# Rows of the late modulation read through GpSimd's DMA queue, and each sum written one part later

## The chip, the cores and the metric

The kernel runs on one core of a Trainium2 chip. The metric is the device time of one execution in microseconds. Three executions of the kernel before took 1044.27, 1046.89 and 1050.75 us; their median is 1046.89 us.

## The reference

One trunk layer of a diffusion backbone: 512 latent tokens and 256 context tokens of width 1024 are modulated, go through two attention branches (latent attention with 8 heads, differential attention with 4), a gated merge and an output projection, a layer norm, and then a routed mixture of 16 experts with a second layer norm. What matters here is the modulation vector:

```
mod = jax.nn.silu(c) @ w_ada[l] + b_ada[l]
sh1, sc1, g1, sh2, sc2, g2 = jnp.split(mod[:, None, :], 6, axis=-1)
...
x = layer_norm(DEEPNORM_ALPHA * x + g1 * o_lat, ln1_g[l], ln1_b[l])
x = layer_norm(DEEPNORM_ALPHA * x + g2 * ec_moe(x * (1.0 + sc2) + sh2, *moe), ln2_g[l], ln2_b[l])
```

w_ada is a 1024 x 6144 matrix in float32. Its first two sixths (sh1, sc1) are needed before anything else. The other four (g1, sh2, sc2, g2) are needed only after the attention; the kernel calls for them later, and they are the "late modulation" of this document.

## The kernel before, in words

**Startup.** The x and ctx tokens are transposed and modulated in four quarters of 256 channels. For each quarter q, `mod_load` (L218) issues on SyncE's queue (SP) the two pieces of w_ada (L222 and L223, tile `wa`, 1 MB each), the tokens (L226, L227, tile `xq`) and the first weight piece of the input projection (L196, tile `wraw`, 512 KB). `mod_mul` (L230) multiplies on TensorE (PE; L237) and VectorE (DVE) copies the result (L240, tile `ms`); `mod_t` turns it into columns (L247 and L250, tiles `scv` and `shv`); `x_chunk` modulates a channel block (L261, tile `xtmp`) and splits it into a high part on ScalarE (ACT; `xlh`, L75) and a low part on GpSimd (POOL; `xll`, L78). Then PE multiplies each block with three passes (L82, L83, L84).

**Projection.** The input projection is done in chunks of up to 512 columns (`chunk`, L362, and `gates`, L447). Each of the four steps of a chunk loads a `wraw` page on SP, splits it into `whi` (ACT) and `wlo` (DVE) and multiplies. Between matmuls the chunks call `mod_chunk` 32 times: 8 times in the chunk C_DV, 12 times in gates(0) and 12 times in gates(1) (table `MOD_AT`, L39).

**Late modulation.** It is done on DVE. A part is one block of 128 rows of w_ada and 1024 columns (512 KB, tile `wa2`, shown as `wa_739`, `wa_760` and so on in the orders below). Each part is scaled by its column of silu(c) and added to the running total of the part before (L348; the first part of a sixth by L346). Eight parts give a sixth, and there are four such sixths, 32 parts. After the eighth part `mod_sum` (L353) sums over the 128 rows with four matmuls on PE (L358), loads 64 KB rows of b_ada into a further `wa2` buffer (L359, two DMAs) and adds them on DVE into `rm` (L360). There are three `wa2` buffers (N_WA, L39), for the parts and for the b_ada rows alike. A buffer comes free when its last reader is done: for most parts that is the DVE operation of the next part, for the eighth part of a sixth it is the sum on PE.

**What sets the order.** Up to the attention the framework's scheduler orders each engine's instructions; it may move an instruction past others that it doesn't depend on. Each engine and each DMA queue then runs its own list strictly in order: what stands behind a waiting instruction waits too. In the kernel before, `wraw` pages and `wa2` parts are issued from the same list, SP's. The emission calls of `mod_chunk` first write the sum that is due, then the next part.

**After it.** `mod_end` (L584) transposes `rm` (L589); then come gates(2), gates(3), the attention, the output projection and the experts. From about 520 us on the experts' weights fill the DMA engines.

Of the kernel before, what the change touches and what calls it, by code (L numbers as in the profile page):

```python
# [18 lines left out]
D = 1024  # L19
# [5 lines left out]
KD = D // 128  # L25
# [27 lines left out]
def _layer(tc, A, out, opened):  # L53
    nc = tc.nc
    V, S, G, T = nc.vector, nc.scalar, nc.gpsimd, nc.tensor
    dma = nc.sync.dma_start
# [129 lines left out]
    w_ada = A["w_ada"][0].rearrange("(k p) n -> p k n", p=128)  # L186
# [144 lines left out]
    b_ada = A["b_ada"][0].rearrange("(j n) -> j n", n=512)  # L331
    wrt = mw.tile([128, KD, E_N], F32, name="wrt")
    halves, late = [], []

    def mod_chunk():

        for fn in late:
            fn()
        late.clear()
        if len(halves) == 4 * KD:  # L340
            return
        j, k = divmod(len(halves), KD)
        wa = mw.tile([128, D], F32, name="wa2", bufs=N_WA)
        dma(wa, w_ada[:, k, (2 + j) * D:(3 + j) * D])
        if k == 0:
            V.tensor_scalar(wa, wa, cs[:, 0, 0:1], None, op0=OP.mult)  # L346
        else:
            V.scalar_tensor_tensor(wa, wa, cs[:, k, 0:1], halves[-1], op0=OP.mult, op1=OP.add)  # L348
        halves.append(wa)
        if k == KD - 1:  # L350
            late.append(lambda: mod_sum(j, wa))

    def mod_sum(j, wa):  # L353
        i, h = divmod(j, 2)
        pm = psa.tile([128, 512], F32, name="tp", bufs=2)
        bm = mw.tile([128, D], F32, name="wa2", bufs=N_WA)
        for g in (2 * h, 2 * h + 1):
            T.matmul(pm[32 * g:32 * g + 32, :], one2[:, 0:1].to_broadcast([128, 32]), wa[:, (g % 2) * 512:(g % 2) * 512 + 512], start=True, stop=True)  # L358
            dma(bm[32 * g:32 * g + 32, :512], b_ada[4 + 4 * i + g:5 + 4 * i + g].to_broadcast([32, 512]))  # L359
        V.tensor_tensor(rm[i][64 * h:64 * h + 64], pm[64 * h:64 * h + 64], bm[64 * h:64 * h + 64, :512], op=OP.add)  # L360

    def chunk(col, n, cuts, evac, at, nxt):  # L362
# [257 lines left out]
    while len(halves) < 4 * KD or late:  # L620
        mod_chunk()
# [276 lines left out]
    for c in range(4):  # L898
        hl = wos[c]
        for jj in range(2):  # L900
            j = 2 * c + jj
            ps = psc.tile([128, 512], F32, name="om", bufs=3)
            wo_mul(ps, hl, jj, oM)
            g = yt.tile([128, 512], F32, name="gy")
# [485 lines left out]
```

## Time and profile before

| | |
|---|---|
| median of three runs | 1046.89 us |
| the profiled execution's own time | 1044.37 us |
| its span, first to last instruction | 1042.6 us |
| mean granted TensorE clock | 0.986 of full speed |
| PE busy | 980.1 us (94% of the span) |
| DVE busy | 447.2 us (43%) |
| ACT busy | 278.3 us (27%) |
| POOL busy | 173.4 us (17%) |
| w_ada parts of the late modulation | 32 DMAs of 512 KB on SP, median 4.6 us to landing |

Issuing a DMA from SP isn't counted as busy time; "to landing" is the time from the start of the issue to the arrival of the last byte's signal. A granted clock of 1.00 is the 2.4 GHz level; a stretch with 0.92 ran partly at 1.2 GHz. A busy time of PE includes the overlap of pipelined matmuls, so a full PE may be below its peak.

### The profile page before, as it was taken

What the parts mean: (1) busy time and instruction counts of PE and PEld (TensorE: products, weight loads), DVE (VectorE), ACT (ScalarE), POOL (GpSimd) and SP (SyncE); (2) the same over time, 40 slices, a digit from 0 to 9 for tenths busy, and PEclk for the clock granted to TensorE, in tenths of its full rate; (3) what the DMA queues carried; (4) which work ended last, traced back from release to release, by engine and by line L of the source; (5) the groups of instructions that cost most, each with busy time, mean ns of one, the idle gap of its engine ahead of it and who ended that gap; (6) DMA issues with size and microseconds to landing.
All of it is one profiled execution on the core that took longest, in us unless ns stands there. A gap on an engine that the chain in (4) does not pass through costs nothing.

```text
span 1042.6 us, 13825 instructions
## 1 busy us (share of the span) xinstructions
PE 980.1 (94%) x5280; PEld 615.3 (59%) x5280; DVE 447.2 (43%) x871; ACT 278.3 (27%) x556; POOL 173.4 (17%) x176
## 2 busy tenths in 40 slices
PE   6999999999989999999996999999999999999982
PEld 5888977768778777777764443535353534234331
DVE  2382366662678555558473312221313131111227
ACT  1222325224777555544110101010101010010010
POOL 2340020202677322210021400000000000000004
PEclk9999999999999999999998999999999999999997
DMA  9944347752111100038948989999999999999993
GB/s 299 289 157 131 96 119 257 239 189 78 27 35 57 41 1 21 21 99 300 406 161 325 376 303 408 409 409 409 409 408 409 409 409 409 409 409 409 410 371 118
DMA packets 101210, 266.98 MB, mean 256 GB/s; under 512 B 14020, under 2 KB 37528, under 8 KB 101144
## 3 DMA queue, kind: packets, MB, share of 16 engines
q1 hardware_dynamic: 100248, 264.52, 68.2%
q0 software_dynamic: 320, 1.05, 0.3%
q8 instruction: 42, 0.69, 0.3%
q10 hardware_dynamic: 576, 0.52, 0.1%
q14 instruction: 24, 0.20, 0.1%
HBM read 261.47 MB, written 2.10 MB: 253 GB/s over the span
## 4 chain that ended last, share of the span: by engine, by line
PE 70%; DMA 10%; issue 9%; DVE 5%; POOL 2%; ACT 2%; SPq 0%; POOLq 0%; DVEq 0%; ACTq 0%
PE h L1179 15%; PE y L1195 8%; PE mx L1142 6%; PE acc L82 5%; PE acc L84 5%; PE acc L83 5%; DMA wr<-moe_w 5%; PE sc L653 4%; DMA wa<-w_ada 3%; PE tpb L661 3%; PE av L841 3%; PE mx L1208 2%; PE po L84 1%; PE po L83 1%; PE po L82 1%
## 5 line engine op out<-in xcount | busy, mean ns | idle before, releaser
L1179 PE MATMUL h<-wr,xe 128*64 128x512 f32 x1024 | 233.6, 598 | 8.9 <-DMA wr<-moe_w 7.9
L1179 PEld LDWEIGHTS h<-wr,xe 128*64 128x64 f32 x1024 | 68.2, 136 | 163.0 <-issue 106.6
L1195 PE MATMUL y<-wr,hidT 128*64 128x512 f32 x448 | 97.7, 594 | 0.0
L642 DVE TENSOR_REDUCE nm<-sc 128x1 f32<-128x768 f32 x64 | 61.0, 953 | 34.4 <-PE sc L653 33.8
L1182 DVE TENSOR_TENSOR hid<-hid,h 128x512 f32<-128x512 f32 x16 | 11.0, 688 | 147.8 <-PE h L1179 147.8
L1195 PEld LDWEIGHTS y<-wr,hidT 128*64 128x64 f32 x448 | 31.5, 137 | 61.8 <-issue 58.2
L1154 POOL TENSOR_TENSOR oh<-oh,aff 128x512 f32<-128x512 f32 x8 | 8.4, 1048 | 350.2 <-PE mx L1142 350.2
L643 ACT ACTIVATE P<-sc,nm 128x768 f32<-128x768 f32 x64 | 57.6, 901 | 31.8 <-DVE nm L642 22.7
L1142 PE MATMUL mx<-oh,xn 128*128 128x128 f32 x512 | 60.4, 280 | 1.4 <-DVE oh L1132 1.4
L1142 PEld LDWEIGHTS mx<-oh,xn 128*128 128x128 f32 x512 | 59.4, 196 | 2.5 <-issue 1.3
L75 ACT ACTIVATE whi<-wraw 128x1024 fp32r<-128x1024 f32 (+1 forms) x32 | 33.5, 1046 | 100.8 <-DMA wraw<-w_in 76.8
L78 DVE TENSOR_TENSOR wlo<-wraw,whi 128x1024 fp32r<-128x1024 f32 (+1 forms) x32 | 38.7, 1209 | 45.0 <-PE acc L83 29.1
L75 ACT ACTIVATE ye<-y 128x512 fp32r<-128x512 f32 (+2 forms) x17 | 9.7, 572 | 178.1 <-DVE y L1202 98.7
L82 PE MATMUL acc<-xlh,whi 128*128 128x512 f32 x128 | 51.6, 403 | 2.8 <-ACT whi L75 2.0
L1209 DVE TENSOR_TENSOR acc<-acc,mx 128x512 f32<-128x512 f32 x56 | 34.7, 680 | 41.4 <-PE mx L1208 41.4
L1181 ACT ACTIVATE hid<-h 128x512 f32<-128x512 f32 x16 | 9.6, 597 | 154.9 <-PE h L1179 154.9
L83 PE MATMUL acc<-xll,whi 128*128 128x512 f32 x128 | 50.8, 397 | 0.0
L82 PE MATMUL acc<-whi,xlh 128*128 128x512 f32 (+1 forms) x128 | 49.5, 391 | 1.0 <-ACT whi L75 1.0
L84 PE MATMUL acc<-xlh,wlo 128*128 128x512 f32 x128 | 50.0, 398 | 0.0
L1202 DVE SCALAR_TENSOR_TENSOR y<-y,gate,g2b 128x512 f32<-128x512 f32 x14 | 9.9, 754 | 92.6 <-PE y L1195 92.6
L84 PE MATMUL acc<-whi,xll 128*128 128x512 f32 (+1 forms) x128 | 48.7, 381 | 0.5 <-POOL xll L78 0.5
L83 PE MATMUL acc<-wlo,xlh 128*128 128x512 f32 (+1 forms) x128 | 48.8, 381 | 0.2 <-DVE wlo L78 0.2
(341 smaller groups left out, 1704.4 us busy)
## 6 DMA issues: line engine op xcount, KB each, us to landing
wr<-moe_w SPq DMA_DIRECT2D x372, 512.0 KB, 10.2
wa<-w_ada SPq DMA_DIRECT2D x32, 512.0 KB, 4.6
wraw<-w_in SPq DMA_DIRECT2D x28, 512.0 KB, 4.8
wa<-w_ada SPq DMA_DIRECT2D x8, 1024.0 KB, 9.8
wr<-moe_w SPq DMA_DIRECT2D x16, 384.0 KB, 8.4
outraw<-w_out SPq DMA_DIRECT2D x8, 512.0 KB, 11.1
xq<-x SPq DMA_DIRECT2D x4, 512.0 KB, 7.8
q<-q SPq DMA_DIRECT2D x16, 128.0 KB, 2.3
```

Source lines behind the costliest of these rows:

```text
L75: S.activation(hi, src, AF.Copy)
L78: (eng_lo or V).tensor_tensor(lo, src, f(hi), op=OP.subtract)
L82: T.matmul(ps, lh, rh, start=start, stop=False)
L83: T.matmul(ps, lh, rl, start=False, stop=False)
L84: T.matmul(ps, ll, rh, start=False, stop=stop)
L642: V.tensor_reduce(nm, ps[:, :768], axis=AX.X, op=OP.max, negate=True)
L643: S.activation(p, ps[:, :768], AF.Exp, bias=nm, accum_out=z)
L653: T.matmul(ps[:, a:b], l, r[:, a:b], start=i == 0, stop=i == len(passes) - 1)
L1142: T.matmul(pss[hf][:, kk * 128:(kk + 1) * 128], xn[t][:, k * 128:(k + 1) * 128], o[:, t].rearrange("p e s -> p (e s)"), start=t == 0, stop ...
L1179: T.matmul(ph[i][64 * hf:64 * hf + 64, :], xe[:, k, sl], w[:, hf * 512:(hf + 1) * 512], start=k == 0, stop=k == KD - 1)
L1195: T.matmul(py[hf][r0:r0 + 64, :], hT[:, e % 2, fc % 4, fc // 4, :], w[:, hf * 512:(hf + 1) * 512], start=fc == 0, stop=fc == KD - 1)
L1209: V.tensor_tensor(acc[t][:, hs], acc[t][:, hs], ps, op=OP.add)
```

## The change

`mod_chunk` now writes the next part first and the sum that was due after it, so a sum is written one part later than before. The 32 loads of parts (512 KB each) and the 8 loads of b_ada rows are issued from GpSimd's queue instead of SP's. Nothing else differs.

```
     def mod_chunk():
 
-        for fn in late:
+        due = late[:]
+        late.clear()
+        if len(halves) < 4 * KD:
+            mod_part()
+        for fn in due:
             fn()
-        late.clear()
-        if len(halves) == 4 * KD:
-            return
+
+    def mod_part():
         j, k = divmod(len(halves), KD)
         wa = mw.tile([128, D], F32, name="wa2", bufs=N_WA)
-        dma(wa, w_ada[:, k, (2 + j) * D:(3 + j) * D])
+        G.dma_start(wa, w_ada[:, k, (2 + j) * D:(3 + j) * D])
         if k == 0:
             V.tensor_scalar(wa, wa, cs[:, 0, 0:1], None, op0=OP.mult)
         else:
...
-            dma(bm[32 * g:32 * g + 32, :512], b_ada[4 + 4 * i + g:5 + 4 * i + g].to_broadcast([32, 512]))
+            G.dma_start(bm[32 * g:32 * g + 32, :512], b_ada[4 + 4 * i + g:5 + 4 * i + g].to_broadcast([32, 512]))
```

From this place on the line numbers of the changed kernel are 3 higher: L346 and L348 become L349 and L351, the load L344 becomes L347, the sum L358 becomes L361.

The scheduler puts the instructions elsewhere. DVE's list at the start of the program, before; `cs` is silu(c), `ms`, `vecs`, `scv`, `shv` and `xtmp` belong to the first quarter of the startup:

```order
L168 TENSOR_SCALAR cs<-sg 128x8
L169 TENSOR_SCALAR cs<-sg 128x8
L240 COPY ms<-tp 128x128
L183 COPY vecs<-tp 128x68
L184 TENSOR_SCALAR gsub<-vecs 128x1
L247 SCALAR_TENSOR_TENSOR scv<-tp,vecs 128x4
L250 TENSOR_TENSOR shv<-tp,vecs 128x4
```

And the same place in the changed kernel:

```order
L169 TENSOR_SCALAR cs<-sg 128x8
L349 TENSOR_SCALAR wa_739<-wa_739,cs 128x1024
L351 SCALAR_TENSOR_TENSOR wa_760<-wa_760,cs,wa_739 128x1024
L240 COPY ms<-tp 128x128
L183 COPY vecs<-tp 128x68
L351 SCALAR_TENSOR_TENSOR wa_787<-wa_787,cs,wa_760 128x1024
L184 TENSOR_SCALAR gsub<-vecs 128x1
L247 SCALAR_TENSOR_TENSOR scv<-tp,vecs 128x4
```

The first two parts of the late modulation now stand ahead of `ms`, the third ahead of `scv`; six more (up to `wa_904` and `wa_1366`, the first part of the next sixth) stand among the second quarter's and ahead of the third quarter's `ms`. Before, the first part stood behind all four quarters.

DVE's list at the second quarter in the changed kernel, where four of these parts stand among the quarter's own steps:

```order
L351 SCALAR_TENSOR_TENSOR wa_808<-wa_808,cs,wa_787 128x1024
L351 SCALAR_TENSOR_TENSOR wa_835<-wa_835,cs,wa_808 128x1024
L240 COPY ms<-tp 128x128
L351 SCALAR_TENSOR_TENSOR wa_856<-wa_856,cs,wa_835 128x1024
L247 SCALAR_TENSOR_TENSOR scv<-tp,vecs 128x4
L250 TENSOR_TENSOR shv<-tp,vecs 128x4
L351 SCALAR_TENSOR_TENSOR wa_883<-wa_883,cs,wa_856 128x1024
L261 TENSOR_SCALAR xtmp<-tp,scv,shv 128x512
```

In the kernel before, these rows hold `ms`, `scv`, `shv` and `xtmp` alone.

SP's list before, around the end of the second sixth (parts up to `wa_1460`, its b_ada rows in `wa_1476`, then the third sixth from `wa_1482`):

```order
L344 DMA wa_1451<-w_ada 128x1024
L471 DMA wuq<-mla_w_uq 128x768
L196 DMA wraw<-w_in 128x2x512
L344 DMA wa_1460<-w_ada 128x1024
L359 DMA wa_1476<-b_ada 32x512 x2
L344 DMA wa_1482<-w_ada 128x1024
L344 DMA wa_1497<-w_ada 128x1024
```

POOL's list in the changed kernel at the same place (the third sixth begins with `wa_1475`, the b_ada rows are in `wa_1479`; `qtok` are short additions of the latent queries):

```order
L347 DMA wa_1451<-w_ada 128x1024
L347 DMA wa_1460<-w_ada 128x1024
L347 DMA wa_1475<-w_ada 128x1024
L362 DMA wa_1479<-b_ada 32x512 x2
L347 DMA wa_1497<-w_ada 128x1024
L347 DMA wa_1506<-w_ada 128x1024
L502 TENSOR_TENSOR qtok<-q1t,q2t 128x2x32 x2
L347 DMA wa_1521<-w_ada 128x1024
```

The weight loads (`wraw`, `wuq`) no longer stand among the parts. The two b_ada loads now come behind the first part of the next sixth, and so take the buffer that the DVE operation of `wa_1460` frees.

## Rows read from the trace of the kernel before

**Rows 1.** Busy time by stretch of the span (its header names the columns).
```profile
core 0: us, PE busy (x) PEld busy (x) DVE busy (x) ACT busy (x) POOL busy (x), PEclk, DMA share, GB/s
0.00:26.00 26.00, 17.10 (x167) 13.96 (x168) 6.53 (x22) 4.32 (x7) 6.18 (x13) 1.00 0.92 299
26.00:52.00 26.00, 25.53 (x223) 21.02 (x222) 8.41 (x16) 7.11 (x11) 8.86 (x8) 1.00 0.98 289
52.00:143.00 91.00, 91.00 (x449) 79.01 (x449) 43.52 (x70) 26.56 (x55) 16.91 (x17) 1.00 0.41 124
143.00:160.00 17.00, 17.00 (x83) 13.22 (x81) 13.26 (x20) 4.66 (x7) 3.80 (x6) 1.00 0.52 160
160.00:180.00 20.00, 18.29 (x84) 14.51 (x83) 13.46 (x21) 10.98 (x39) 0.14 (x1) 1.00 0.74 257
180.00:200.00 20.00, 19.19 (x89) 15.62 (x90) 15.39 (x43) 4.75 (x13) 6.58 (x16) 1.00 0.70 237
200.00:212.00 12.00, 9.97 (x41) 7.24 (x40) 6.49 (x7) 3.87 (x6) 0.00 (x0) 0.97 0.76 245
212.00:230.00 18.00, 18.00 (x77) 13.65 (x76) 11.40 (x16) 4.21 (x6) 1.15 (x1) 0.92 0.69 223
```

**Rows 2.** Chain that ended last, in order of time: start us, us, what.
```profile
150.11 0.98 PE tp L358 x4
...
152.16 4.59 DMA wa<-w_ada
156.84 1.30 DVE wa L348
...
168.60 4.83 DMA wa<-w_ada
173.52 1.29 DVE wa L348
174.86 1.05 PE tp L358 x4
...
225.21 0.98 PE tp L358 x4
```

**Rows 3.** What SP's queue waited for, 0 to 260 us: total us, times, longest.
```profile
SPq L344 <- DVE wa L348: 56.3, 21, 6.3
SPq L344 <- PE tp L358: 9.0, 3, 7.0
```

**Rows 4.** What PE waited for, 140 to 262 us: total us, times, longest.
```profile
PE acc L82 <- ACT whi L75: 2.0, 1, 2.0
PE tp L358 <- DVE wa L348: 1.5, 1, 1.5
```

**Rows 5.** Operations on tile wa: ns min/median/max, first and last start, forms.
```profile
L348 DVE SCALAR_TENSOR_TENSOR wa<-wa,cs,wa x28: 1276/1285/1758, 62.9 to 223.6; 128x1024 f32<-128x1024 f32 x28
```

**Rows 6.** Line L344, the parts' loads on SP: issue to landing.
```profile
DMA to landing us min/median/max: 3.5/4.6/5.0
```

**Rows 7.** DVE in order of time, startup: start, us, instruction, idle before it.
```profile
11.90 0.29 DVE L240 COPY ms<-tp 128x128 f32<-128x128 f32 x1 [7.98 <-PE tp L237]
12.62 0.16 DVE L247 SCALAR_TENSOR_TENSOR scv<-tp,vecs 128x4 f32<-128x4 f32 x1
24.81 0.29 DVE L240 COPY ms<-tp 128x128 f32<-128x128 f32 x1 [7.11 <-PE tp L237]
27.71 1.48 DVE L261 TENSOR_SCALAR xtmp<-tp,scv,shv 128x512 f32<-128x512 f32 x2 [0.97 <-PE tp L258]
29.11 1.22 DVE L78 TENSOR_TENSOR wlo<-wraw,whi 128x1024 fp32r<-128x1024 f32 x1
```

**Rows 8.** Line L1217, the only loads issued from POOL (256 KB each).
```profile
L1217 POOL DMA_DIRECT2D gb<-ln_g x2: 589/673/757, 565.6 to 571.8; - x2
L1217 POOL DMA_DIRECT2D gb<-ln_b x2: 546/552/559, 566.4 to 572.4; - x2
...
DMA to landing us min/median/max: 6.1/6.5/7.8
```

**Rows 9.** POOL in order of time, startup.
```profile
14.64 1.27 POOL L78 TENSOR_TENSOR xll<-xtmp,xlh 128x512 fp32r<-128x512 f32 x1 [12.72 <-ACT xlh L75]
...
29.26 2.20 POOL L78 TENSOR_TENSOR xll<-xtmp,xlh 128x512 fp32r<-128x512 f32 x1 [9.72 <-ACT xlh L75]
```

## The prediction, made before the changed kernel ran

> **What bounds the kernel now.** I first read the busy time by stretch [rows 1]. Three regimes are to be seen there up to 230 us. From 0 to 52 us the DMA engines are busy 0.92 and 0.98 of the time at 299 and 289 GB/s, and PE lacks 8.9 us of the first stretch: the startup waits for transfers. From 52 to 160 us PE is full. From 160 to 212 us PE lacks 1.71 + 0.81 + 2.03 = 4.55 us, and from 200 to 230 us its granted clock is 0.97 and 0.92, part of the time at the lower of its two levels, which costs 12 x 0.03 + 18 x 0.08 = 1.8 us. What could be won by a better late modulation is therefore about 6.3 us: nothing before 160 us has a gap but the startup.
>
> The chain that ended last says what the gap is [rows 2]. Between the first sum of the late modulation (150.11 us) and the last (225.21 us), 75.1 us, it runs through loads of parts and their DVE operations: 4.59 us, 1.30 us, later 4.83 us, 1.29 us, then the sum on PE. The waits agree: SP's queue stood 56.3 us over the parts' loads until a DVE operation freed a buffer, and 9.0 us until a sum freed one [rows 3], while PE itself waited 1.5 us for a sum's input and 2.0 us for a split weight page [rows 4]. So the late stretch has its own clockwork, with three buffers: a load may start when the operation two parts earlier is done. Two parts take a landing and an operation.
>
> Its size can be checked. From one sum to the next there are four such links, of a landing of 4.6 us (the median of these loads [rows 6]) and an operation of 1.285 us [rows 5], and about 1 us for the sum [rows 2]: 4 x 5.9 + 1 = 24.6 us. Three intervals make 73.7 us, against 75.1 us seen. PE's own work in this stretch is a little less than that, so the clockwork and PE run almost together. The landing time of a part is thus the quantity that decides: 12 landings stand one behind the other.
>
> **The change: the startup.** With its own queue, the first part no longer waits behind SP's list. The order shows nine parts, 9 x 0.524 = 4.7 MB, ahead of or among the first three quarters of the startup, where DVE had none. DVE runs in order, so what matters is not only whose bytes go first. The copy `ms` of the first quarter can't run until the operations of two parts are done, and `scv` not until a third is. Whatever the share of the two queues, 3 x 0.524 = 1.57 MB more must have landed by then. At 299 GB/s [rows 1] that is 5.3 us. The first two operations fit in the 7.98 us in which DVE waits before `ms` [rows 7]; the third lies between `vecs` and `scv`, on the path to the first `xtmp`: 1.3 us. In the second quarter `ms` came at 24.81 us and `xtmp` at 27.71 us [rows 7]; two more operations stand between them, one of which fits beside the transposes PE does there, the other not: 1.3 us. Loads four to seven must land in the some 13 us between the two `ms`; I count them as hidden by PE's work on the first quarter. Sum: 5.3 + 1.3 + 1.3 = 7.9 us. PE has no gap from 26 to 160 us but 0.47 us [rows 1], so nothing gives this back. The bounds: at least the 1.3 us of the third operation, if the loads fitted in idle DMA time; that is 0.08 x 26 + 0.02 x 26 = 2.6 us of it in 52 us, 0.8 MB, so they don't. At most all nine loads in series, 4.7 MB at 299 GB/s, 15.8 us.
>
> **The change: the middle.** The DVE operations and loads that leave the stretch from 52 to 143 us lay beside a full PE [rows 1]; I count 0.
>
> **The change: the late stretch.** The nine early parts don't start the clockwork earlier. The eleventh load takes over either a buffer that the first sum on PE reads or one freed after it, and that sum keeps its place in the last part of PE's work before 151 us. So 23 parts remain between the first and the last sum, with the same three buffers, and the same 12 landings in series. Two terms change.
>
> First, the landing of a load issued from POOL. The only ones in the trace are four loads of half the size, in the stretch in which the expert weights flow: 6.1 to 7.8 us [rows 8]. The nearest on the other side are the parts' own loads on SP: 3.5 us at best, 4.6 us in the median [rows 6]. So a landing lies between 3.5 and 7.8 us. The new queue has no weight page ahead of a part, and the stretch's DMA share is 0.69 to 0.76 [rows 1], not full as at the expert weights; but the issue alone holds POOL for 0.55 to 0.76 us [rows 8]. I take the middle of 4.6 and 6.1 us, 5.35 us: 12 x 0.75 = 9.0 us more.
>
> The Trainium skill speaks for less. Its page "DMA: Bandwidth & Descriptors", section "Anatomy of one DMA — SWDGE (gpsimd) path", gives 2.0 us plus bytes over 436 GB/s for a DMA issued from GpSimd, an estimate of 3.2 us for a part. By it the first rival below would hold. The trace does not agree where it shows such loads: 6.1 us for 256 KB [rows 8].
>
> Second, the b_ada loads. Before, they were issued while the eighth part was still on its way. Now the sum is written a part later, and they wait for the buffer that the eighth part's operation frees; the next sixth's second load stands behind both of them on POOL. Two issues of 0.6 us [rows 8] at two of the sums: 2.4 us. The additions `qtok` also stand behind loads on POOL now, but their readers come in the attention.
>
> What is removed: a weight page no longer waits on SP behind a part, so PE's 2.0 us for a split page goes [rows 4]. What is late next is the sum, whose wait grows by the same amount. I count 0, as I do for the 4.55 us of gaps: they return only if the clockwork gets shorter than PE's work.
>
> **The sum.** 7.9 + 9.0 + 2.4 = 19.3 us. Added to the profiled execution's own time, 1044.37 us (its span of 1042.6 us and 1.8 us around it), this gives 1063.7 us; I say 1064 us. That execution is 2.5 us below the median of the three runs, well inside their spread. The later stages start with what the attention leaves and run as before, so the shift carries through to the end. With a startup of 5 to 10 us and a landing of 4.6 to 6.1 us this case runs from 1044.4 + 5 + 0 + 2.4 = 1052 to 1044.4 + 10 + 18 + 2.4 = 1075 us.
>
> **The rivals.** *Not slower: the freed queue makes the clockwork shorter than PE's work.* Place: the parts' loads between the sums. If a landing is the 3.5 us of the quiet loads [rows 6], an interval is 4 x 4.8 + 1 + 1.2 = 21.4 us, while PE's busy time between the sums is about 23.5 us ([rows 1]: 18.29 + 19.19 in 40 us, and 9.97 in 12). PE then bounds it and gets back 6.3 us; with the startup's 7.9 us that is 1046 us, and if the startup's loads hid as well, 1038 us. It decides from a landing under about 4.0 us. For it: the new queue holds no weight pages. Against it: [rows 8].
>
> *Only the startup pays.* A part lands as on SP, 4.6 us, and the b_ada loads hide: 1044.4 + 7.9 = 1052 us. For it: the check of the clockwork above, which needs nothing else. Against it: POOL's issues are longer than SP's.
>
> *Much slower: POOL's loads are held up.* With the 7.8 us of [rows 8] as landing the late stretch grows by 12 x 3.2 = 38 us, 1093 us with the rest. A mechanism for it is seen at the startup: POOL's low part took 2.20 us instead of 1.27 us [rows 9] where DVE's `wlo`, with two inputs in SBUF, ran beside it from 29.11 us [rows 7]. The operation of a part has two such inputs as well. If each of the 12 issues in series were held for one operation, that is 12 x 1.3 = 15 us on top of the forecast, 1079 us. The Trainium skill's page "SBUF — State Buffer" has the rule ("DVE blocks DMA", and section "Who interferes with whom"): DVE and GpSimd share a port pair, and descriptors of a GpSimd DMA wait for it. It limits the clash for two-input operations to GpSimd instructions that read SBUF; no run here shows descriptors written beside one.
>
> *The change doesn't do what it says.* The sums are written later, but the scheduler places three of the four a few matmuls earlier on PE, not later; so what the later writing does is only the b_ada term, already counted.
>
> **How the numbers follow.** A measurement of this kernel tells about 1% from no change, that is under 1036.4 or over 1057.4 us against the median. My forecast has 0.52, only the startup 0.17, not slower 0.15, much slower 0.16. Of the forecast about 0.44 lies over 1057.4 us, with much slower 0.16 and 0.02 of the second rival: 0.62. Faster by over 1% needs both the whole 6.3 us and a free startup: 0.03. The rest, 0.35, is within 1%. The range leaves out most of the much slower case and half of the not slower one: 1048 to 1080 us.
>
> **What would show it.** In the changed profile: L349 and the first L351 before the first `ms`, with DVE waiting for them or `ms` later than 11.90 us by some 5 us, and the second quarter's `xtmp` at about 36 us; DMA share near 1 until after 50 us; PE full from there to the first sum, now at about 158 us; landings of L347 near 5.4 us; first to last sum about 86 us instead of 75.1; POOL as the releaser of DVE's waits. I am wrong if the first sum still comes by 152 us (startup hidden), or if the stretch between the sums is no longer than 75 us.

## The result, and the profile after

The changed kernel takes 1065.15 us in the median of four executions (1060.49 to 1066.07 us), the kernel before 1046.2 us in the median of four beside it. The ratio is 1.0155, with a 95% interval of 1.0128 to 1.0183: slower by 1.3 to 1.8%. Its profiled execution took 1065.24 us with a span of 1063.2 us, 20.6 us above that of before; the mean granted TensorE clock is 0.977 of full speed where it was 0.986.

Four marks in PE's timeline divide the loss. "First scores" is the first product of queries and keys after the projections.

| us from the start | before | after | later by | added here |
|---|---|---|---|---|
| first sum of the late modulation | 150.1 | 158.1 | 8.0 | 8.0 |
| last sum | 225.2 | 238.7 | 13.5 | 5.5 |
| first scores | 262.4 | 280.1 | 17.7 | 4.2 |
| scores of the other branch (L653, L656) | 330.6 | 349.8 | 19.2 | 1.5 |
| end of the span | 1042.6 | 1063.2 | 20.6 | 1.4 |

So 17.7 us are lost before the attention, in two places: the startup, and the stretch of the late modulation. Some 3 us come later, and no run here was made for them.

**The startup.** Busy time by stretch of the changed kernel, answering to [rows 1]:

```profile
core 0: us, PE busy (x) PEld busy (x) DVE busy (x) ACT busy (x) POOL busy (x), PEclk, DMA share, GB/s
0.00:26.00 26.00, 13.39 (x99) 10.26 (x101) 10.70 (x26) 4.43 (x7) 9.18 (x18) 1.00 0.94 324
26.00:52.00 26.00, 23.68 (x205) 19.30 (x206) 13.28 (x19) 5.19 (x8) 8.90 (x12) 0.93 1.07 361
52.00:143.00 91.00, 91.00 (x500) 79.30 (x499) 29.30 (x55) 26.84 (x56) 17.04 (x18) 1.00 0.32 85
...
160.00:180.00 20.00, 19.18 (x85) 15.46 (x83) 12.81 (x13) 8.36 (x21) 3.58 (x8) 1.00 0.89 317
180.00:200.00 20.00, 15.94 (x67) 13.01 (x67) 11.64 (x30) 7.94 (x33) 6.21 (x13) 0.83 0.54 175
...
230.00:245.00 15.00, 9.76 (x36) 6.41 (x35) 8.02 (x7) 1.06 (x1) 2.09 (x4) 0.77 0.41 138
```

The DMA engines were nearly full before, at 299 and 289 GB/s; now they bring 324 and 361 GB/s, and still PE is busy 3.7 us less in the first 26 us and 1.9 us less in the next; there its granted clock is also 0.93 instead of 1.00, which is worth 26 x 0.07 = 1.8 us. These three make 7.4 of the 8.0 us. After 52 us PE is full again, with nothing given back. The later lines show where PE falls behind a second time: 4.1 us idle in the 20 us from 180 us, 5.2 us in the 15 us from 230 us, both with the granted clock partly at the lower level (0.83 and 0.77).

VectorE in the first two quarters of the startup of the changed kernel, answering to [rows 7] (start, us, instruction, idle before it and its releaser):

```profile
7.82 0.75 DVE L349 TENSOR_SCALAR wa<-wa,cs 128x1024 f32<-128x1024 f32 x1 [3.91 <-DMA wa<-w_ada]
9.89 1.28 DVE L351 SCALAR_TENSOR_TENSOR wa<-wa,cs,wa 128x1024 f32<-128x1024 f32 x1 [1.32 <-DMA wa<-w_ada]
16.42 0.29 DVE L240 COPY ms<-tp 128x128 f32<-128x128 f32 x1 [5.25 <-PE tp L237]
16.77 1.28 DVE L351 SCALAR_TENSOR_TENSOR wa<-wa,cs,wa 128x1024 f32<-128x1024 f32 x1
18.02 0.15 DVE L247 SCALAR_TENSOR_TENSOR scv<-tp,vecs 128x4 f32<-128x4 f32 x1
...
29.25 0.29 DVE L240 COPY ms<-tp 128x128 f32<-128x128 f32 x1 [1.85 <-PE tp L237]
33.51 1.29 DVE L351 SCALAR_TENSOR_TENSOR wa<-wa,cs,wa 128x1024 f32<-128x1024 f32 x1 [3.96 <-DMA wa<-w_ada]
...
35.23 1.28 DVE L351 SCALAR_TENSOR_TENSOR wa<-wa,cs,wa 128x1024 f32<-128x1024 f32 x1 [0.29 <-DMA wa<-w_ada]
36.43 0.80 DVE L261 TENSOR_SCALAR xtmp<-tp,scv,shv 128x512 f32<-128x512 f32 x1
```

The first `ms` comes at 16.42 us instead of 11.90, and what it waited for last is PE's product (5.25 us), which waits for the first sixths' rows of w_ada: that is transfer time. `scv` then stands behind a part's operation of 1.28 us. In the second quarter DVE waits 3.96 us for a part while the quarter's own steps stand behind it, and the second quarter's `xtmp` comes at 36.43 us, where it came at 27.71.

**The late stretch.** What PE waited for in the changed kernel from 140 to 262 us, answering to [rows 4] (total us, times, longest):

```profile
PE tp L361 <- DVE wa L351: 10.6, 3, 5.2
PE acc L82 <- DVE q2t L499: 1.0, 1, 1.0
```

PE stands 10.6 us in front of three of the four sums, where it stood 1.5 us. Both kernels have one and the same thing to wait for, the operation on the eighth part. The 9.1 us more are about the 5.5 + 4.2 = 9.7 us that the table adds behind the first sum. The chain that ended last, in the same stretch (start, us, what), answering to [rows 2]:

```profile
158.16 1.00 PE tp L361 x4
...
175.53 1.30 DVE wa L351
176.83 0.28 issue
177.12 4.49 DMA wa<-w_ada
181.70 1.29 DVE wa L351
183.13 1.92 PE tp L361 x4
...
189.68 0.70 DVE rm L363
190.38 0.29 issue
190.67 0.46 POOL wa L347
...
232.72 4.49 DMA wa<-w_ada
237.31 1.29 DVE wa L351
238.65 1.92 PE tp L361 x4
```

It is the clockwork of before, a load, an operation, a load, an operation, with two things new. Between an operation and the load that it lets go stand 0.28 us. And two of the three sums that PE waited for, those after 3.95 and 5.24 us, take 1.92 us instead of 1.05: the granted clock is 0.50 there, the 1.2 GHz level. The one after 1.41 us takes 1.05 us.

Around the second sum the trace also shows how a wait of PE comes back to the parts. GpSimd, ScalarE and VectorE there (start, us, instruction, idle before it and its releaser):

```profile
183.27 1.01 POOL L362 DMA_DIRECT2D wa<-b_ada  x2 [3.03 <-DVE wa L351]
185.35 0.58 POOL L347 DMA_DIRECT2D wa<-w_ada  x1 [1.06 <-PE tp L361]
186.67 0.79 ACT L481 ACTIVATE vm<-acc 128x128 f32<-128x128 f32 x4 [5.53 <-PE acc L84]
188.42 1.22 DVE L78 TENSOR_TENSOR wlo<-wraw,whi 128x1024 fp32r<-128x1024 f32 x1 [3.29 <-ACT whi L75]
189.68 0.69 DVE L363 TENSOR_TENSOR rm<-tp,wa 64x512 f32<-64x512 f32 x1
```

While PE stands at the sum, ScalarE waits 5.53 us for PE's products (`vm`); the split `whi` stands behind them, the split `wlo` on VectorE waits for `whi`, and the sum's addition `rm` stands behind `wlo`. It starts 4.6 us after the sum is done, and only then the buffer of the b_ada rows goes to the load at 190.67 us. In the kernel before the addition follows the second sum at once, at 175.96 us.

The landing of a part is not what grew. Loads of parts in the changed kernel from 140 to 260 us (first line: ns of the issue, first and last start; then what GpSimd waited for in front of them, us and times; then issue to landing), answering to [rows 3, 6]:

```profile
L347 POOL DMA_DIRECT2D wa<-w_ada x23: 537/543/606, 159.4 to 232.7; - x23
...
  DVE wa L351: 30.2, 12
  DVE rm L363: 8.3, 3
...
DMA to landing us min/median/max: 3.8/4.4/5.8
```

A median of 4.4 us here, and of 4.6 us over all 32 loads, is SP's own 4.6 us (of SP's 32 loads the trace has a landing for 11).

### The profile page after: what moved, and what is told of

It is laid out like the page before. It is cut to its first block, busy times and chain, and to the rows that moved or that the text cites. A ratio compares the mean times of both kernels' runs of the same rounds, so it can differ in the third digit from the quotient of the medians.

```text
span 1063.2 us, 13832 instructions
## 1 busy us (share of the span) xinstructions
PE 987.4 (93%) x5280; PEld 620.1 (58%) x5280; DVE 447.1 (42%) x871; ACT 278.3 (26%) x556; POOL 195.9 (18%) x216
## 4 chain that ended last, share of the span: by engine, by line
PE 68%; issue 11%; DMA 11%; DVE 5%; POOL 3%; ACT 2%; SPq 0%; POOLq 0%; DVEq 0%; ACTq 0%
PE h L1182 14%; PE y L1198 8%; DMA wr<-moe_w 6%; PE mx L1145 6%; PE acc L84 5%; PE acc L83 5%; PE acc L82 5%; PE sc L656 4%; DMA wa<-w_ada 4%; PE tpb L664 3%; PE av L844 2%; PE mx L1211 2%; PE po L84 1%; PE po L83 1%; PE po L82 1%
## 5 line engine op out<-in xcount | busy, mean ns | idle before, releaser
L351 DVE SCALAR_TENSOR_TENSOR wa<-wa,cs,wa 128x1024 f32<-128x1024 f32 x28 | 36.8, 1315 | 31.3 <-DMA wa<-w_ada 31.1
```

## The experiments

The median time, the ratio to the kernel before with its 95% interval, and from the profile: first and last sum, PE's wait in front of the sums, first scores (all us). The first two rows are the two kernels' profiles from above.

| run | first sum | last sum | PE waits at sums | first scores | median us | ratio |
|---|---|---|---|---|---|---|
| before | 150.1 | 225.2 | 1.5 | 262.4 | 1046.2 | 1 |
| after | 158.1 | 238.7 | 10.6 | 280.1 | 1065.15 | 1.0155 (1.0128 to 1.0183) |
| e1 order alone | 150.4 | 227.5 | 1.2 | 263.8 | 1050.65 | 1.0011 (0.999 to 1.0031) |
| e2 queue alone | 164.7 | 246.4 | 12.7 | 288.1 | 1075.05 | 1.0248 (1.0222 to 1.0274) |
| e3 start held | 150.6 | 233.5 | 13.6 | 275.0 | 1059.71 | 1.0102 (1.0077 to 1.0126) |
| e4 rows in place | 172.3 | 235.7 | 5.7 | 284.1 | 1071.21 | 1.0218 (1.019 to 1.0247) |
| e5 held, rows in place | 169.3 | 235.0 | 6.9 | 283.4 | 1067.82 | 1.0174 (1.0129 to 1.0218) |
| e6 rows in place, SP | 160.4 | 219.9 | 0.7 | 266.3 | 1053.5 | 1.005 (1.0028 to 1.0072) |
| e7 early loads, late products | 155.7 | 236.8 | 11.8 | 277.5 | 1062.01 | 1.0127 (1.0086 to 1.0167) |
| e8 held, b_ada on SP | 150.2 | 235.4 | 12.0 | 273.6 | 1059.23 | 1.0084 (1.006 to 1.0108) |
| e9 SP, issued late | 149.7 | 233.7 | 1.3 | 264.2 | 1048.86 | 1.0001 (0.9979 to 1.0023) |
| e10 only first loads on GpSimd | 158.5 | 233.5 | 2.0 | 269.8 | 1058.66 | 1.009 (1.0061 to 1.0118) |
| e11 held, one copy | 149.9 | 242.5 | 15.6 | 277.3 | 1064.47 | 1.015 (1.0101 to 1.0199) |
| e12 held, two copies | 150.3 | 248.9 | 13.3 | 274.9 | 1064.27 | 1.0137 (1.0097 to 1.0177) |

**e1: the order alone.** The changed kernel with all loads back in SP's queue.

```diff
-        G.dma_start(wa, w_ada[:, k, (2 + j) * D:(3 + j) * D])
+        dma(wa, w_ada[:, k, (2 + j) * D:(3 + j) * D])
...
-            G.dma_start(bm[32 * g:32 * g + 32, :512], ...
+            dma(bm[32 * g:32 * g + 32, :512], ...
```

> The sums are written one part later, all loads stay on SP. Theory (two causes: parts pulled into the startup by the new queue, and b_ada rows that now wait for the eighth part's operation): the startup is that of before, first sum at 150 to 151 us; the b_ada rows stand on SP behind the eighth part's operation, so the stretch from the first to the last sum grows from 75.1 us by 2 to 5 us; 1047 to 1053 us. Rival (the queue alone is the cause, the order is harmless): 75 us between the sums, 1044 to 1047 us.

Measured: no difference from the kernel before is seen, ratio 1.0011 (0.999 to 1.0031). The first sum is at 150.4 us, the stretch grew by 2.0 us to 77.1 us, the low end of the theory, and PE waits 1.2 us at the sums. Writing the sums a part later costs 0.3% at most. The loss belongs to the queue.

**e2: the queue alone.** The kernel before with its order, the 32 parts and 8 b_ada loads in GpSimd's queue.

```diff
-        dma(wa, w_ada[:, k, (2 + j) * D:(3 + j) * D])
+        G.dma_start(wa, w_ada[:, k, (2 + j) * D:(3 + j) * D])
...
-            dma(bm[32 * g:32 * g + 32, :512], ...
+            G.dma_start(bm[32 * g:32 * g + 32, :512], ...
```

> The 40 loads go through POOL, the sums are written where they were before. Theory: the nine parts still move into the startup, so the first sum comes at 158 us; without the later writing the b_ada rows no longer wait for the eighth part, and the stretch between the sums keeps 75 to 78 us; 1052 to 1058 us. Rival (the whole loss is the queue's): as the changed kernel, 80 us between the sums, 1062 to 1066 us.

Measured: 1075.05 us, worse than the whole change, which I had not expected, and outside both ranges. Between the sums lie 81.7 us, as the rival had it. Here the startup alone costs 14.6 us. VectorE of this kernel in front of the third quarter shows why:

```profile
43.05 1.29 DVE L348 SCALAR_TENSOR_TENSOR wa<-wa,cs,wa 128x1024 f32<-128x1024 f32 x1 [1.95 <-DMA wa<-w_ada]
52.17 0.75 DVE L346 TENSOR_SCALAR wa<-wa,cs 128x1024 f32<-128x1024 f32 x1 [7.84 <-DMA wa<-w_ada]
52.84 0.28 DVE L240 COPY ms<-tp 128x128 f32<-128x128 f32 x1
```

The third quarter's `ms` is ready to run, but the ninth part's operation stands ahead of it and waits 7.84 us for its load. That load went out only at 44.63 us. In the old order the two b_ada loads stand before it on GpSimd and take, at 37.65 us, the buffer that the seventh part's operation freed; the ninth part's load gets the next one, which the eighth part's operation frees at 43.05 + 1.29 = 44.34 us. (Four splits of the input stand before it as well, but GpSimd was done with them at 43.13 us.) In the changed kernel the ninth part's load takes the first of these buffers and is issued at 36.80 us, and this `ms` comes at 46.79 us. So within the new queue the later sums save 6.6 us of the startup (first sum at 158.1 instead of 164.7 us); with SP's queue (e1) no such help is seen.

**e3: the start held.** The changed kernel, but the first part's load has to stand behind GpSimd's last split of the input.

```diff
-        (eng_lo or V).tensor_tensor(lo, src, f(hi), op=OP.subtract)
+        return (eng_lo or V).tensor_tensor(lo, src, f(hi), op=OP.subtract)
...
-        split(dh[:, k, :], dl[:, k, :], tm[:, :w], eng_lo=G)
+        last_x.append(split(dh[:, k, :], dl[:, k, :], tm[:, :w], eng_lo=G))
...
-        G.dma_start(wa, w_ada[:, k, (2 + j) * D:(3 + j) * D])
+        with tc.issue_after(last_x[-1].ins):
+            G.dma_start(wa, w_ada[:, k, (2 + j) * D:(3 + j) * D])
```

> The changed kernel, with the parts' loads held behind POOL's last split of the startup, so that no part is loaded before about 60 us. Theory: the first sum returns to 150 to 151 us and the 8 us of the startup come back, the rest stays: 1055 to 1058 us. Rival (the startup's delay is absorbed or has another cause): 1062 to 1066 us, first sum later than 155 us.

Measured: the first load goes out at 62.9 us, the first sum is back at 150.6 us, and the time falls to 1059.71 us, between the two ranges. The startup's loss is thus the early loads, and undoing them is worth 0.5% (1.0155 to 1.0102, 5.5 us). The rest, 1.0%, stays: PE now waits 13.6 us at the sums.

**e4: the b_ada rows land in the sum's own tile.** With this a sum takes no third row buffer from the parts.

```diff
-        bm = mw.tile([128, D], F32, name="wa2", bufs=N_WA)
...
-            G.dma_start(bm[32 * g:32 * g + 32, :512], ...
+            G.dma_start(rm[i][32 * g:32 * g + 32], ...
-        V.tensor_tensor(..., pm[64 * h:64 * h + 64], bm[64 * h:64 * h + 64, :512], op=OP.add)
+        V.tensor_tensor(..., pm[64 * h:64 * h + 64], rm[i][64 * h:64 * h + 64], op=OP.add)
```

> The changed kernel, with the b_ada rows loaded straight into the tile rm that receives the sum, so that they take no wa2 buffer and the next part waits for neither them nor rm. Theory: the startup still costs 8 us; the stretch between the sums falls under 75 us, as the parts run ahead of the sums; 1048 to 1056 us. Rival (POOL's loads themselves are what is slow): the stretch stays at 78 us or more, 1060 to 1066 us.

Measured: the time, 1071.21 us, missed both ranges. The stretch from first to last sum is 63.4 us instead of 80.6, so the buffer was one of the things that parts waited for. But the parts that became free ran ahead into the startup, and the first sum is 22 us later than before. VectorE of this kernel at the third and fourth quarter:

```profile
54.99 1.28 DVE L351 SCALAR_TENSOR_TENSOR wa<-wa,cs,wa 128x1024 f32<-128x1024 f32 x1 [6.74 <-DMA wa<-w_ada]
56.19 0.28 DVE L240 COPY ms<-tp 128x128 f32<-128x128 f32 x1
63.03 1.28 DVE L351 SCALAR_TENSOR_TENSOR wa<-wa,cs,wa 128x1024 f32<-128x1024 f32 x1 [3.67 <-DMA wa<-w_ada]
69.40 1.29 DVE L351 SCALAR_TENSOR_TENSOR wa<-wa,cs,wa 128x1024 f32<-128x1024 f32 x1 [3.23 <-DMA wa<-w_ada]
74.15 0.29 DVE L240 COPY ms<-tp 128x128 f32<-128x128 f32 x1 [2.32 <-PE tp L237]
```

`ms` of the third quarter waits through 6.74 us of a part's transfer, and that of the fourth comes at 74.15 us (59.92 us in the changed kernel). A shorter stretch is not a faster kernel.

**e5: both edits, held start and rows in place; e6: rows in place alone, in the kernel before, on SP.** If the parts could not reach the startup, the shorter stretch might beat the kernel before.

> The changed kernel with both earlier edits at once: the late rows' loads wait for GpSimd's last split of the input, and the b_ada rows land in the sum's own tile, so that a sum needs no third row buffer. Theory (the loss is parts pulled into the start, plus a late stretch in which a sum takes a row buffer from the parts): the first sum stands at about 150.6 us, as with the hold alone, and the stretch from the first to the last sum is under 72 us where the hold alone had 82.9 (the same edit took 17 us from the stretch of the changed kernel); the first product of scores by about 258 us and the time 1038 to 1047 us, at or under the kernel before. Rival (GpSimd's queue is the slow part, whatever the buffers): the stretch stays over 78 us and the time at 1055 us or more.

> The kernel before with only the b_ada rows landing in the sum's own tile; all loads in the weights' queue. Theory: the start is as before (first sum at 150 us), and the stretch to the last sum is shorter than the 75.1 us of before, if the row buffer that a sum holds was what its parts waited for; the time 1035 to 1045 us. Rival (the parts come in step with the weights' loads, which stand in the same queue, so that a free buffer buys nothing): the stretch within 2 us of 75.1 and the time 1044 to 1050 us.

Both missed: 1067.82 and 1053.5 us. The parts now run ahead into the stretch from 100 to 143 us, in which PE had been full. What PE waited for from 50 to 175 us, in e5:

```profile
PE acc L83 <- DVE wlo L78: 10.5, 3, 5.9
```

and in e6:

```profile
PE acc L83 <- DVE wlo L78: 6.3, 3, 3.5
```

`wlo`, the low part of a weight page, stands on VectorE behind operations that wait for parts (37.0 us of such waits in e5 between 50 and 175 us). It is the startup's loss at another place. In e6 PE waits only 0.7 us at the sums, the last of them is 5.3 us earlier than before, and the first scores are still 3.9 us later. No version here beats the kernel before.

**e7: three early loads, no early products.** Which share of the startup's loss is bytes, and which is VectorE's order? The loads stay early; the first part's operation must stand behind the last `xtmp`.

```diff
+        xv = V.tensor_scalar(tm[:, :w], px[:, :w], scv[:, k, ci:ci + 1], ...
+        last_x.append(xv)
...
-            V.tensor_scalar(wa, wa, cs[:, 0, 0:1], None, op0=OP.mult)
+            with tc.issue_after(last_x[-1].ins):
+                V.tensor_scalar(wa, wa, cs[:, 0, 0:1], None, op0=OP.mult)
```

> The changed kernel with its loads left early in GpSimd's queue, but the first part's product on VectorE held until the last piece of the input is scaled: three row buffers, so three loads (1.57 MB) still land in the start, and no VectorE operation stands between the quarters. Theory A (bytes: the start is as long as what the DMA engines have to bring): the first sum still comes at 155 us or later and the time is 1060 us or more. Theory B (VectorE works in order and waited for parts in front of the quarters' own work): the first sum is back at 150 to 152.5 us and the time near the 1059.7 us of the held loads, 1055 to 1061 us.

Measured: first sum at 155.7 us and 1062.01 us, as theory A had it, so three loads of 0.524 MB cost 5.6 us with no operation of theirs near the quarters. VectorE of this kernel:

```profile
16.12 0.29 DVE L241 COPY ms<-tp 128x128 f32<-128x128 f32 x1 [12.07 <-PE tp L238]
...
29.82 0.29 DVE L241 COPY ms<-tp 128x128 f32<-128x128 f32 x1 [7.92 <-PE tp L238]
32.70 1.47 DVE L262 TENSOR_SCALAR xtmp<-tp,scv,shv 128x512 f32<-128x512 f32 x2 [0.96 <-PE tp L259]
```

The first `ms` is nearly as late as in the changed kernel (16.12 against 16.42 us), the second quarter's `xtmp` is at 32.70 us between 27.71 and 36.43. The remaining 2.4 us of the 8.0 at the first sum are, by subtraction, the operations among the quarters and the later early loads; no run parts these two.

**e8: held start, b_ada rows back on SP.** Are the two b_ada loads per sum, which stand in front of the next part's load on GpSimd, the late stretch's loss?

```diff
...
-            G.dma_start(bm[32 * g:32 * g + 32, :512], ...
+            dma(bm[32 * g:32 * g + 32, :512], ...
```

> The changed kernel with the parts' loads held behind the last split of the input, in GpSimd's queue, and the b_ada rows' loads back in the weights' queue. Theory (the rest of the loss, 7.8 us between the first and the last sum, comes from the sum's b_ada loads standing in front of the next part's load in GpSimd's queue while they wait for a buffer): the stretch falls from 82.9 us to 75 to 78 us and the time to 1046 to 1053 us. Rival (it comes from the place of the sum's addition on VectorE behind the weights' split, whichever queue brings the rows): the stretch stays at 81 us or more and the time at 1057 us or more.

Measured: 1059.23 us against e3's 1059.71, and 85.2 us between the sums. Taking the b_ada loads out of GpSimd's queue wins nothing (on SP they now wait 20.2 us for the eighth parts' operations, with weight pages behind them, but PE waits for no weight page). PE in e8:

```profile
PE tp L363 <- DVE wa L353: 12.0, 3, 6.1
```

The rival's numbers came. Its reason, the place of the sum's addition behind the weights' split, is seen in the trace: the addition starts 4.6 us after the second sum, as in the changed kernel and in e3, where e1 has 2.6 us. No run moved it, so this rival stays open.

e1 and e8 differ, behind the startup, in the queue of the parts' loads and in what the scheduler makes of it, and that is worth 0.7% of the time (1.0084 against 1.0011) and 9.8 us at the first scores.

**e9: SP's queue, made to issue late.** What differs per load is small. Two operations and the loads that they release; in the kernel before:

```profile
167.29 1.28 DVE L348 SCALAR_TENSOR_TENSOR wa<-wa,cs,wa 128x1024 f32<-128x1024 f32 x1
...
168.60 0.33 SPq L344 DMA_DIRECT2D wa<-w_ada  x1
```

and in the changed kernel:

```profile
163.50 1.29 DVE L351 SCALAR_TENSOR_TENSOR wa<-wa,cs,wa 128x1024 f32<-128x1024 f32 x1 [2.19 <-DMA wa<-w_ada]
...
165.08 0.54 POOL L347 DMA_DIRECT2D wa<-w_ada  x1 [4.06 <-DVE wa L351]
```

167.29 + 1.28 = 168.57, so SP issues 0.03 us after the operation ends; 163.50 + 1.29 = 164.79, so GpSimd issues 0.29 us after it. Over the 23 loads of the stretch the medians of this gap are 0.03 and 0.30 us. e9 is e1 with a copy of no use in SP's list ahead of each part's load from the 18th part on; it reads the result of the operation that the load waits for.

```diff
+        if len(halves) > 16:
+            pad = mw.tile([8, 16], F32, name="pad", bufs=4)
+            dma(pad, halves[-2][:8, :16])
         dma(wa, w_ada[:, k, (2 + j) * D:(3 + j) * D])
```

> The changed kernel's order with all loads in the weights' queue (the run of the order alone: 77.1 us between the first and the last sum, 1050.6 us), and in the late stretch one copy of 8x16 elements issued ahead of each part's load, waiting for the same product: it does no work but puts the load's issue about 0.33 us after the product that frees its buffer, where that queue needs 0.03 us and GpSimd's needs 0.30 us. Theory (the late stretch is a ring of loads and products in two row buffers at a time, and what GpSimd's queue costs there is only that it issues 0.27 us later and 0.2 us longer, on every turn of the ring): the stretch grows from 77.1 to 81 to 86 us, as far as with GpSimd's queue (82.9 and 85.2 us with the start held), and the time to 1055 to 1062 us. Rival (0.3 us for each load is absorbed by slack, and the loss lies in something else of GpSimd's queue): the stretch stays under 79.5 us and the time under 1053 us.

Measured: the gap became 0.73 us in the median, more than twice what was planned, on the 15 loads that have a copy. The stretch grew to 84.1 us, as far as with GpSimd's queue: half of the theory, but with the larger gap it does not show that 0.27 us a load would have been enough. But the time did not grow at all, 1.0001 (0.9979 to 1.0023): the rival's half, though not for its reason, since slack did not absorb the delay. PE in e9:

```profile
PE tp L364 <- DVE wa L354: 1.3, 1, 1.3
```

The sums came nearly as late as in e8 and PE did not stand still for them. The program's list shows a reason. PE's order is fixed when the program is built, and with the copies in it the scheduler counted the parts as later: the third and fourth sum stand in rows 775 and 881 of PE's list, where the order alone has 771 and 863, e8 772 and 868, and the changed kernel 768 and 857. PE had other matmuls to do first. So late sums by themselves cost nothing here; what e8 loses and e9 does not is PE's wait in front of them.

**e10: only the first nine loads on GpSimd.** The startup's loss by itself, the late loads on SP.

```diff
-        G.dma_start(wa, w_ada[:, k, (2 + j) * D:(3 + j) * D])
+        (G.dma_start if len(halves) < 9 else dma)(wa, w_ada[:, k, (2 + j) * D:(3 + j) * D])
...
-            G.dma_start(bm[32 * g:32 * g + 32, :512], ...
+            dma(bm[32 * g:32 * g + 32, :512], ...
```

> The changed kernel with only its first nine parts' loads in GpSimd's queue; the later ones and the b_ada rows' in the weights' queue. Theory (two losses that add up: about 8 us of the start, and what the queue costs in the late stretch): the first sum at 157 to 159 us, the stretch from the first to the last sum back at 75 to 78 us, the time 1054 to 1059 us. Rival (the late stretch is long because the start was late, so that parts and weights meet otherwise, not because of the queue): the stretch stays at 80 us or more and the time at 1061 us or more.

Measured: first sum at 158.5 us, 75.0 us between the sums, 1058.66 us, all as the theory had it; PE:

```profile
PE tp L361 <- DVE wa L351: 2.0, 2, 1.2
```

The two losses can be had apart: this run has the first without the second, e3 and e8 the second without the first. The first alone is worth 0.90%, the second alone 1.02% (e3) and 0.84% (e8), the whole change 1.55%: the sum, less some 3 us, which is about what PE waits less at the sums in the changed kernel than in e3 (10.6 against 13.6 us).

**e11 and e12: sums placed later on PE, loads on GpSimd.** If PE's place for the sums is the loss, copies as in e9 in GpSimd's list, from the tenth part on, should cure it: the scheduler places the sums later. e11 has one copy ahead of a load, e12 two, both on e3.

```diff
+        if len(halves) > 8:
+            for _ in range(2):
+                pad = mw.tile([8, 16], F32, name="pad", bufs=4)
+                G.dma_start(pad, halves[-2][:8, :16])
```

> The changed kernel with its start held, and from the tenth part on one copy of 8x16 elements ahead of each part's load in GpSimd's queue: no work, but the program's order, which is fixed when it is built, now counts the parts as later and puts the sums 5, 12 and 28 rows later on TensorE (rows 662, 778 and 883 where the held kernel has 657, 766 and 855). The parts themselves come later too. Theory (what the late stretch costs is TensorE standing still in front of sums that the order puts ahead of their parts: 13.6 us in the held kernel): the stretch between the first and the last sum grows (over 84 us where it was 82.9), and yet TensorE's wait at the sums falls to 3 to 9 us, the first product of scores comes at 265 to 271 us where it was 275.0, and the time is 1049 to 1057 us where it was 1059.7. Rival (the lateness of the parts itself is the loss, wherever the sums stand): the first product of scores at 275 us or later and the time 1060 us or more.

> The same with two such copies ahead of each part's load: the sums stand at rows 671, 803 and 919 of TensorE's order, 14, 37 and 64 rows later than in the held kernel. Theory: TensorE's wait at the sums is under 6 us, the first product of scores at 263 to 271 us and the time 1047 to 1057 us, though the stretch between the first and the last sum is the longest of all, over 88 us. Rival (lateness of the parts is the loss): later and slower than the run with one copy, the time 1062 us or more.

Both missed. The stretches are 92.7 and 98.6 us, and PE's wait did not fall: in e11

```profile
PE tp L367 <- DVE wa L357: 15.6, 3, 7.2
```

and 13.3 us in e12. On GpSimd the copies delayed the parts by as much as the sums were moved, or more. The rival's numbers fit e11 (277.3 and 1064.47 us); for e12 it wanted a run later and slower than e11, and it is neither (274.9 and 1064.27 us, with a stretch 5.9 us longer). What does agree in all runs with the buffers of before is the bookkeeping: take the first scores of the kernel before, add the shift of the first sum and the extra wait of PE at the sums. For e2 that gives 262.4 + 14.6 + 11.2 = 288.2 us (288.1 measured), for e3 275.0 (275.0), e8 273.0 (273.6), e7 278.3 (277.5), e12 274.4 (274.9), after 279.5 (280.1), and at worst, e9, 261.8 (264.2). Sums that stand later without making PE wait change nothing. A cure, sums placed later on PE without later parts, was not found, so that the place of the sums is the loss rests on e9 and this bookkeeping.

## Why the prediction was right, point by point

The direction, the size (1064 us forecast, 1065.15 measured, inside the likeliest case's 1052 to 1075) and the first term were right; the two other terms came out right in sum and wrong in cause. That the total fits to about 1 us is luck in this part: the prediction had 9.0 + 2.4 = 11.4 us behind the first sum from two causes that the runs don't show, and measured are 9.7 us up to the first scores and 12.6 us up to the end of the span.

- **The startup, 7.9 us: right, 8.0 us at the first sum.** Its split held too, as far as it can be seen. The 1.57 MB of three parts were put at 5.3 us; e7 shows 5.6 us for those three loads. The two operations were put at 2.6 us; 2.4 us are left for them and for the six later loads, with the lower clock from 26 to 52 us, which the prediction did not have, somewhere in these sums. The second quarter's `xtmp`, forecast at about 36 us, came at 36.43. "Nothing gives this back" held up to the first sum; at the end of the program holding the loads (e3) gave 5.5 us, since PE then waits 3 us more at the sums, as if a late start were a little slack for the parts.
- **The middle, 0: right.** PE is full from 52 to 143 us, 91.00 of 91.00 us, as before.
- **The landings, 9.0 us: this step failed.** It read "I take the middle of 4.6 and 6.1 us, 5.35 us: 12 x 0.75 = 9.0 us more", from loads issued on GpSimd in the experts' stretch [rows 8]. The runs show 4.4 us in this stretch, no longer than SP's [rows 6]. The nearest row was nearest in its queue and far in what else moved: those loads share the DMA engines with the experts' weights. What makes the late stretch longer instead is, as far as shown, the gap between an operation and the load that it releases, 0.30 us for 0.03. On 12 turns in series that is 3.2 us. Runs with the late loads on GpSimd have more than that between the sums: 5.6 us more than their counterpart on SP in the changed kernel (against e10, which starts alike), 5.8 in e3 (against e1), 6.6 in e2 (against the kernel before), 8.1 in e8 (against e1). So 2.4 to 4.9 us are not shown to be the gap, and their cause stays open. The traces show two things that may be in them, neither tried by itself: landings (medians of 4.9 us in e2 and 4.7 in e8, against 4.4 to 4.6 on SP), and the way in which a wait of PE holds back the sum's addition and with it the next load (4.6 us from the second sum to its addition in the changed kernel, e3 and e8, 2.6 in e1, 3.0 in e10). The second can't be all: in e2 the addition follows at once.
- **The b_ada loads, 2.4 us: not seen.** At the second sum the two issues are over at 184.28 us, and the next part's load goes out at 185.35 us, 0.30 us after the sum on PE (183.13 + 1.92 = 185.05 us) has freed its buffer. At the third it goes out at 213.84 us, 0.6 us after the end of the sum, so some 0.3 us may be the issues' where the prediction had 1.2 us at each of two sums. With these loads on SP (e8) the ratio is 1.0084 against 1.0102 with them on GpSimd (e3), inside both intervals, which could not tell 2.4 us (0.2%) from nothing.
- **What the prediction did not have: PE's order.** It computed how long the clockwork takes and put the whole growth on the path. By e9 a growth of 7 us costs nothing if the sums' places on PE grow with it. In the changed kernel the second to fourth sums stand at 659, 768 and 857 of PE's list, where the kernel before has 665, 771 and 858. A row can hold several matmuls; counted singly it is 8 or 9 matmuls earlier, about 2 us at the 0.23 us from one to the next. The last sum's parts come 5.5 us later, counted from the first sum, and PE no longer waits 2.0 us for a split page [rows 4] and so is there earlier, as the prediction had said. These three make about the 9.1 us of added waiting. The prediction saw those places ("the scheduler places three of the four a few matmuls earlier on PE, not later") and used them only to dismiss a rival. It also looked for 86 us between the sums; they are 80.6 us apart, and another 4.2 us fall behind the last sum, where PE starts again at the lower clock level (0.77 from 230 to 245 us) and where some matmuls more are left to do, since the sum stands earlier.
- **The rivals.** "Only the startup pays" had the landing right, a part lands as on SP, and is refuted by e3: without the startup's loss 1.0102 remains. "Not slower" asked for a landing under about 4.0 us; it is 4.4. "Much slower" by a port held against GpSimd: the issues in the late stretch take 537 to 606 ns and the landings at most 5.8 us, and 13 of the 23 issues run beside a VectorE operation with two inputs in SBUF, so nothing of 1.3 us per load is seen. The Trainium skill's page "SBUF — State Buffer", section "Who interferes with whom", had been cited for it; read with its limit to instructions that read SBUF the page and this trace agree.
- **The signs.** Three of those it named did not come: landings near 5.4 us, 86 us between the sums, and POOL as the releaser of VectorE's waits. VectorE waited for the loads themselves (3.96 us in the second quarter). And of the 56.3 us that it read from [rows 3] for the late stretch, 35.3 us lie between 152 and 245 us.

The estimate from the Trainium skill's page "DMA: Bandwidth & Descriptors", section "Anatomy of one DMA — SWDGE (gpsimd) path", 3.2 us for a part, lies under all landings measured on GpSimd here (3.8 us at least). The measurement decides; but the page's direction, a shorter landing than the forecast took, was the better one.

## What to carry to other kernels

A queue that has nothing else in it does not only free the old queue: what is loaded there starts as soon as its buffers allow, and each such load, and above all each operation on it that an in-order engine finds ahead of its urgent work, is paid by the stage that happens to run then. So before moving a background stream, ask what held it back until now, and keep that hold (here one dependence on the last urgent instruction brought the first sum back to 150.6 us from 158.1, though not the rest of the loss: that run is still 1.0% slower than the kernel before); and judge a late stream not by when its results come, but by what the engine that reads them has to do in front of them. A price taken from the same queue in a busier stage was here a worse neighbour than one from the other queue in the same stage.

## What was not expected of the hardware

- A load issued from GpSimd landed about as fast as one from SP (512 KB in the late stretch, medians of 4.4 to 4.9 us in the changed kernel, e2, e3 and e8, and of 4.4 to 4.6 us in the kernel before, e1 and e10); the difference is ahead of the issue, 0.30 us after the releasing operation against 0.03, and in the issue itself, 0.54 against 0.33 us.
- The startup moved 361 GB/s from 26 to 52 us in the changed kernel, at a DMA share of 1.07, where it had 289 GB/s at a share of 0.98. The share that the profile gives as full was not the most that the DMA engines could bring. That the second queue did it is not shown: the added loads have rows of 4 KB where the startup's w_ada pieces have rows of 1 KB, and in the experts' stretch of the kernel before SP's queue moves 409 GB/s almost alone.
- PE can pay for a pause a second time. In the changed kernel, after waits of 3.95 and 5.24 us, the four matmuls of a sum took 1.92 us at a granted clock of 0.50, the lower of the two levels; after a wait of 1.41 us, and after none, the same four took 1.05 us. The length of that wait alone does not decide it: in e1 the second sum took 1.92 us after 1.21 us, where PE had waited another 1.47 us shortly before, and in e11 the third took 1.05 us after 2.46 us.
